# Routing one-hots laid out in token pairs, sums laid out by token, and a second stretch without GpSimd: a hybrid decoder layer on one core

## The chip, the cores and the metric

The kernel runs on one core of one Trainium2 chip. The metric is device time in microseconds (us) of one execution. Before the change the median of 3 runs is 2627.22 us (2626.87 to 2627.82).

## The reference, cut to what matters

One decoder layer for 256 tokens of width 2048, all in float32. A first sub-layer (modulated RMSNorm, a convolution branch and a dilated attention branch, an output projection, a residual) is not touched by the change. The second sub-layer is a retrieval of single-neuron experts: for each token, 8 heads choose 16 experts each out of 128 x 128 by product keys, with softmax weights g, and then

```
u = take(w_up, idx)                      # 128 experts of each token
a = gelu(einsum('td,tkd->tk', x, u))
y = einsum('tk,tkd->td', g * a, take(w_down, idx))
```

where `idx = e1 * 128 + e2` and `w_up`, `w_down` are 16384 x 2048.

## The kernel before, in words

The kernel gathers nothing. It computes the up products of all 16384 experts for all 256 tokens, multiplies them by a dense matrix of routing weights C (expert by token, zero where an expert isn't chosen) and multiplies the result by all of `w_down`. The experts are worked in four quarters q of 32 values of e1 (EQ = 32); within one e1, the 128 values of e2 lie on the partitions.

*Float32 by parts.* A weight half of 128 x 1024 is split into `hi` (a float32r copy, ScalarE, line 84) and `lo` (the rest, raw - hi, line 88, on DVE or GpSimd). A product is then three float32r matmuls: hi x hi, hi x lo, lo x hi. In the up products the weights are the stationary operand (lines 1265 to 1267, tile `aps`, 256 columns each); in the down products C is (parts `cch`, `ccl`; lines 1428 to 1431, tiles `y` and `z`, 512 columns each).

*Order.* Work is a list of units of two halves. A `Stream` emits for each half: `a` (for up units a DVE transpose `wt`, then `hi`) three halves ahead, `b` (`lo`, and for down units `cch` and `ccl`) two ahead, and `mm` (the matmuls). What a half carries as `after` is emitted ahead of the next half's `mm`. `hi` has 4 buffers, `lo` 3, `wt` 2, `cch` and `ccl` 3, the raw weight tile 4; a `lo` therefore waits for the matmuls of three halves before. Each engine runs its own instructions in the order of emission. DMA loads of weights are issued by SyncE, when a raw tile comes free.

*Routing weights.* `gate_c(p)` makes C for two quarters, in two passes p of 32 blocks of 8 tokens (NT = 8). Each step of the generator does three things: `apply` for block b-2 (DVE multiplies the sums into C of one quarter, line 1348; ScalarE copies the other quarter's, line 1353), `build` for block b (DVE: `oh2`, line 1328, a one-hot of e2; `oh1`, line 1330, a one-hot of 64 values of e1; `ohg`, line 1333, `oh1` times three bf16 parts of g), and `product` for block b-1 (line 1342: for each of the 8 tokens three matmuls, stationary `oh2` of 128 columns, moving `ohg` of 64 columns, summed over the parts into the PSUM tile `gps`). In the profile `oh1` and `oh2` are both `oh`. The tiles are laid out [.., key, token], with the 8 tokens innermost, so a matmul, which takes one token, reads every eighth bf16 and writes every eighth float32.

*Where the passes lie.* Pass 0 goes beside the 18 "solo" up units of quarter 1, one step after each half; their `lo` are all on GpSimd. I call this the first stretch. Pass 1 goes beside the down units of quarter 1 for the output columns 1024 to 2047 (d == 1), one step after each half, and two steps more in front; all their `lo` are on GpSimd too (in the quarters 0, 2 and 3, d == 1, those of every unit's first half only). I call it the second stretch. The line that chooses, 1407, is

```
split_b(h, u.raw[...], nc.gpsimd if d == 1 and (q == 1 or n == 0) else nc.vector)
```

Of the kernel before, what the change touches and what calls it, by code (L numbers as in the profile page):

```python
# [14 lines left out]
OP = mybir.AluOpType  # L15
# [3 lines left out]
P = 128  # L19
# [14 lines left out]
EQ = 32  # L34
# [32 lines left out]
def layer_kernel(ctx, tc, x, c, norm1_g, norm2_g, w_ada, b_ada, w_in, conv_dw, conv_db, conv_ln_g,  # L67
# [991 lines left out]
    def open_p2():  # L1059
        pool = p2.enter_context(tc.tile_pool(name="p2", bufs=1))  # L1060
        T2["pool"] = pool
        CB[:] = [pool.tile([P, EQ * T], F32, name=f"C{i}") for i in range(2)]
        T2["keys"], T2["keysT"] = CB[0][:, 0:2048], CB[0][:, 2048:4096]
        nc.gpsimd.dma_start(T2["keys"].rearrange("p (a e) -> p a e", a=16),
                            dap(peer_sub_keys, 0, [[P, P], [P * P, 16], [1, P]]))
        T2["scr"] = CB[1]
        it = pool.tile([P, P, 8], BF, name="iota_rep")
        nc.gpsimd.iota(it, pattern=[[1, P], [0, 8]], base=0, channel_multiplier=0, allow_small_or_imprecise_dtypes=True)
        T2["iota"] = it
        T2["e1T"] = pool.tile([P, T], BF, name="e1T")  # L1070
        T2["e2T"] = pool.tile([P, T], BF, name="e2T")
        T2["gp"] = pool.tile([P, 3, T], BF, name="gp")
# [248 lines left out]
    def gate_c(p):  # L1321
        nb = T // NT
        state = {}

        def build(b):
            ts = slice(b * NT, (b + 1) * NT)
            o2 = T2["pool"].tile([P, P, NT], BF, name="oh2", tag="oh2", bufs=2)
            nc.vector.tensor_tensor(o2, T2["iota"], T2["e2T"][:, None, ts].to_broadcast([P, P, NT]), op=OP.is_equal)
            o1 = T2["pool"].tile([P, 2 * EQ, NT], BF, name="oh1", tag="oh1", bufs=1)
            nc.vector.tensor_tensor(o1, T2["iota"][:, 2 * p * EQ:2 * (p + 1) * EQ, :],  # L1330
                                    T2["e1T"][:, None, ts].to_broadcast([P, 2 * EQ, NT]), op=OP.is_equal)
            og = T2["pool"].tile([P, 3, 2 * EQ, NT], BF, name="ohg", tag="ohg", bufs=2)
            nc.vector.tensor_tensor(og, o1[:, None].to_broadcast([P, 3, 2 * EQ, NT]),  # L1333
                                    T2["gp"][:, :, None, ts].to_broadcast([P, 3, 2 * EQ, NT]), op=OP.mult)
            state["o", b] = o2, og

        def product(b):
            o2, og = state.pop(("o", b))
            ps = T2["ps"].tile([P, 2 * EQ, NT], F32, name="gps", tag="m", bufs=2)
            for t in range(NT):  # L1340
                for i in range(3):
                    nc.tensor.matmul(ps[:, :, t], lhsT=o2[:, :, t], rhs=og[:, i, :, t], start=i == 0, stop=i == 2)  # L1342
            state["p", b] = ps

# [35 lines left out]

    def down_unit(q, d, r):

# [9 lines left out]
        for n in range(2):  # L1392
# [11 lines left out]
            def b(h, rr=rr, n=n):  # L1404
                h.ch = T2["pool"].tile([P, T], F32R, name="cch", tag="cch", bufs=3)
                nc.scalar.copy(*row_views(h.ch, q, rr))  # L1406
                split_b(h, u.raw[:, n * 1024:(n + 1) * 1024], nc.gpsimd if d == 1 and (q == 1 or n == 0) else nc.vector)
                h.cl = T2["pool"].tile([P, T], F32R, name="ccl", tag="ccl", bufs=3)
# [4 lines left out]
            def mm(h, rr=rr):  # L1413
# [28 lines left out]
                for t in range(2):  # L1442
                    for c in range(2):
                        products(h, t, c, (0,), first, False)
                    for c in range(2):
                        products(h, t, c, (1,), False, last)

            h.a, h.b, h.mm = a, b, mm
            h.early_b = d == 1
            if rr == EQ - 1 and not (q == 3 and d == 1):  # L1450
                h.after = [lambda: [y_done(q, d, Y["ps"], t, c) for t in range(2) for c in range(2)]]
# [62 lines left out]
    for q in range(4):  # L1514
# [10 lines left out]
        m1 = len(st.halves)  # L1525
        downs = [down_unit(q, 1, r) for r in range(0, EQ, 2)]
        if q == 1:
# [73 lines left out]
```

## Time and profile before

| | |
|---|---|
| median of 3 runs | 2627.22 us |
| profiled execution | 2627.34 us, its span 2625.6 us |
| TensorE busy (matmul / weight load) | 2549.9 us (97%) / 2195.0 us (84%) |
| DVE, ScalarE, GpSimd busy | 1853.8 (71%), 1134.9 (43%), 603.5 us (23%) |
| `gps` matmuls (line 1342) | 1536, recorded mean 303 ns |
| `lo` on GpSimd from raw down weights | 80, mean 2429 ns |
| `ohg`, `oh` of e2, `oh` of e1 on DVE | 64 each, mean 991, 689, 481 ns |
| DMA | 518.74 MB, 198 GB/s over the span |

Matmuls are pipelined and their recorded ends are modelled: a record of 300 ns can be followed by the next start 100 ns later, so the pace is read from starts. "Busy" is a union of such records. A float32 matmul (not float32r) stands as two records. The profile's times are us from the start of the span; "idle before" names what released an instruction.

### The profile page before, as it was taken

The numbers are of one execution on the slowest core, as the hardware profiler recorded it, in microseconds if no ns is written. First come the engines' busy times: TensorE is split into PE (matmuls) and PEld (weight loads), VectorE is DVE, ScalarE is ACT, GpSimd is POOL, SyncE is SP. The second block draws the span as 40 slices with busy tenths as digits, with TensorE's granted clock in tenths as the row PEclk, the third lists the DMA queues.
The fourth block names the chain that finished last, engine by engine and source line by source line (L and its number), as shares of the span: only waits on it lengthen the run. The fifth ranks groups of instructions, "written<-read, shape, count | busy, mean of one in ns | idle before, by whom it ended". The sixth has DMA issues, their size and how long they took to land.

```text
span 2625.6 us, 39801 instructions
## 1 busy us (share of the span) xinstructions
PE 2549.9 (97%) x15760; PEld 2195.0 (84%) x15760; DVE 1853.8 (71%) x2498; ACT 1134.9 (43%) x1493; POOL 603.5 (23%) x294
## 2 busy tenths in 40 slices
PE   7999899999999999999999999999999999999999
PEld 4677677777766999889999988999888999998877
DVE  2655688785554689875568777777787776667776
ACT  5333354445334444432235555555333344445454
POOL 1000000000000038774423243222144211124023
PEclk9999999999999999999999999999999999999999
DMA  9886346777899787774438856889522577765563
GB/s 317 294 294 240 128 145 217 251 273 272 280 304 257 159 179 165 165 157 94 97 94 243 237 198 204 223 227 244 161 97 90 117 185 185 185 187 194 206 212 124
DMA packets 261179, 518.74 MB, mean 198 GB/s; under 512 B 16400, under 2 KB 57568, under 8 KB 260352
## 3 DMA queue, kind: packets, MB, share of 16 engines
q1 hardware_dynamic: 258912, 507.61, 67.3%
q0 software_dynamic: 2048, 8.58, 0.9%
q8 instruction: 123, 2.02, 0.3%
q14 instruction: 64, 0.52, 0.1%
q10 hardware_dynamic: 32, 0.01, 0.0%
HBM read 511.94 MB, written 4.19 MB: 197 GB/s over the span
## 4 chain that ended last, share of the span: by engine, by line
PE 79%; DVE 4%; POOL 2%; issue 2%; ACT 1%; DMA 1%; SPq 0%; DVEq 0%; POOLq 0%; ACTq 0%
PE aps L1267 7%; PE aps L1265 7%; PE aps L1266 7%; PE gps L1342 7%; PE y L1428 6%; PE y L1429 6%; PE y L1431 6%; PE z L429 5%; PE z L431 5%; PE z L430 5%; PE z L1429 3%; PE z L1431 3%; PE z L1428 3%; POOL lo L88 2%; PE ada L330 2%
## 5 line engine op out<-in xcount | busy, mean ns | idle before, releaser
L88 DVE TENSOR_TENSOR lo<-raw,hi 128x1024 fp32r<-128x1024 f32 x432 | 532.9, 1238 | 369.2 <-issue 104.3
L84 ACT CAST hi<-raw 128x1024 fp32r<-128x1024 f32 x512 | 535.0, 1052 | 519.9 <-PE aps L1266 99.2
L1267 PE MATMUL aps<-h2hi,lo 128*128 128x256 f32 x2048 | 581.2, 284 | 8.7 <-POOL lo L88 8.5
L1265 PE MATMUL aps<-h2hi,hi 128*128 128x256 f32 x2048 | 583.1, 285 | 0.4 <-ACT hi L84 0.4
L1266 PE MATMUL aps<-h2lo,hi 128*128 128x256 f32 x2048 | 579.9, 283 | 0.0
L84 ACT CAST hi<-wt 128x1024 fp32r<-128x1024 f32 x256 | 269.5, 1053 | 515.2 <-DVE wt L1250 339.7
L1267 PEld LDWEIGHTS aps<-h2hi,lo 128*128 128x128 f32 x2048 | 392.9, 192 | 11.3 <-POOL lo L88 11.3
L1265 PEld LDWEIGHTS aps<-h2hi,hi 128*128 128x128 f32 x2048 | 393.7, 192 | 2.4 <-ACT hi L84 0.6
L88 POOL TENSOR_TENSOR lo<-wt,hi 128x1024 fp32r<-128x1024 f32 x116 | 288.1, 2490 | 467.5 <-PE aps L1267 354.2
L1266 PEld LDWEIGHTS aps<-h2lo,hi 128*128 128x128 f32 x2048 | 393.3, 192 | 1.8
L1250 DVE STREAM_TRANSPOSE wt<-raw 128x1024 f32<-128x1024 f32 x256 | 315.9, 1237 | 97.7 <-POOL lo L88 85.5
L1411 DVE TENSOR_TENSOR ccl<-C,cch 128x256 fp32r<-128x256 f32 x256 | 258.7, 1012 | 134.8 <-ACT cch L1406 68.6
L88 POOL TENSOR_TENSOR lo<-raw,hi 128x1024 fp32r<-128x1024 f32 x80 | 194.3, 2429 | 423.4 <-PE y L1429 194.0
L1428 PE MATMUL y<-hi,cch 128*128 128x512 f32 x640 | 254.9, 398 | 0.0
L1429 PE MATMUL y<-lo,cch 128*128 128x512 f32 x640 | 250.2, 391 | 0.0
L1342 PE MATMUL gps<-ohg,oh 128*128 128x64 bf16 x1536 | 199.1, 303 | 8.2 <-DVE ohg L1333 8.1
L1342 PEld LDWEIGHTS <-oh 128*128 128x128 bf16 x1536 | 182.3, 147 | 18.0 <-issue 14.4
L1431 PE MATMUL y<-hi,ccl 128*128 128x512 f32 x640 | 197.4, 390 | 0.0
L88 DVE TENSOR_TENSOR lo<-wt,hi 128x1024 fp32r<-128x1024 f32 x140 | 170.9, 1223 | 29.2 <-PE aps L1267 12.5
L1406 ACT CAST cch<-C 128x256 fp32r<-128x256 f32 x256 | 103.1, 403 | 176.3 <-PE z L1429 102.0
L347 POOL TENSOR_TENSOR acc<-acc,raw 128x512 f32<-128x512 f32 x60 | 101.5, 1691 | 262.6 <-ACT raw L346 225.3
L1429 PE MATMUL z<-lo,cch 128*128 128x512 f32 x384 | 149.5, 389 | 2.2 <-DVE lo L88 2.2
(293 smaller groups left out, 4055.2 us busy)
## 6 DMA issues: line engine op xcount, KB each, us to landing
raw<-in_peer_w_up_dram SPq DMA_DIRECT2D x512, 256.0 KB, 5.8
raw<-in_peer_w_down_dram SPq DMA_DIRECT2D x128, 1024.0 KB, 5.1
raw<-in_w_ada_dram SPq DMA_DIRECT2D x86, 1024.0 KB, 7.0
raw<-in_w_in_dram SPq DMA_DIRECT2D x73, 1024.0 KB, 5.3
raw<-in_w_out_dram SPq DMA_DIRECT2D x64, 256.0 KB, 5.1
raw<-in_peer_w_q_dram SPq DMA_DIRECT2D x64, 256.0 KB, 6.5
raw<-in_w_in_dram SPq DMA_DIRECT2D x22, 512.0 KB, 8.8
raw<-in_w_ada_dram SPq DMA_DIRECT2D x20, 512.0 KB, 5.1
```

What stands on the lines that cost most here:

```text
L84: nc.scalar.copy(h.hi, src)
L88: eng.tensor_tensor(h.lo, src, h.hi.bitcast(F32), op=OP.subtract)
L429: nc.tensor.matmul(z, lhsT=ah, rhs=hi[:, kk], start=first, stop=False)
L1250: nc.vector.transpose(wt.rearrange("p j g a -> p g j a"), u.raw.rearrange("p (g j a) -> p g j a", g=4, a=32)[:, :, n * 8:(n + 1) * 8, :])
L1265: nc.tensor.matmul(z, lhsT=hi[:, jj], rhs=qh["hi"][:, j, :], start=j == 0, stop=False)
L1266: nc.tensor.matmul(z, lhsT=hi[:, jj], rhs=qh["lo"][:, j, :], start=False, stop=False)
L1267: nc.tensor.matmul(z, lhsT=lo[:, jj], rhs=qh["hi"][:, j, :], start=False, stop=j == NK - 1)
L1342: nc.tensor.matmul(ps[:, :, t], lhsT=o2[:, :, t], rhs=og[:, i, :, t], start=i == 0, stop=i == 2)
L1411: nc.vector.tensor_tensor(cl, row, ch, op=OP.subtract)
L1428: nc.tensor.matmul(z, lhsT=ch, rhs=hi, start=first, stop=False)
L1429: nc.tensor.matmul(z, lhsT=ch, rhs=lo, start=False, stop=False)
L1431: nc.tensor.matmul(z, lhsT=cl, rhs=hi, start=False, stop=last)
```

## The change

Three edits.

1. The one-hot tiles are laid out [block of two tokens, key, 2 tokens] instead of [key, 8 tokens]; `iota_rep` shrinks from 8 to 2 copies. A matmul now reads every second bf16. `ohg` is made by three instructions, one for each part of g, instead of one.
2. The PSUM tile `gps` is laid out [token, 64 values of e1] instead of [64 values, token]; a matmul writes 64 neighbouring float32, and `apply` reads through a transposed view.
3. In the second stretch (q == 1, d == 1) all `lo` go to DVE, and every fourth row (r % 4 == 2, n == 1: rows 3, 7, ..., 31) has no `hi`, `lo`, `cch` and `ccl`: its four products are plain float32 matmuls of C and the raw weights, and the raw tile is released by them.

```
-        it = pool.tile([P, P, 8], BF, name="iota_rep")
+        it = pool.tile([P, P, 2], BF, name="iota_rep")
...
+            pairs = lambda v: v.rearrange("p (b t) -> p b t", t=2)
+            nb2, ne = NT // 2, 2 * EQ
+            o2 = T2["pool"].tile([P, nb2, P, 2], BF, name="oh2", tag="oh2", bufs=2)
+            nc.vector.tensor_tensor(o2, T2["iota"][:, None].to_broadcast([P, nb2, P, 2]),
+                                    pairs(T2["e2T"][:, ts])[:, :, None].to_broadcast([P, nb2, P, 2]), op=OP.is_equal)
+            o1 = T2["pool"].tile([P, nb2, ne, 2], BF, name="oh1", tag="oh1", bufs=1)
...
+            og = T2["pool"].tile([P, 3, nb2, ne, 2], BF, name="ohg", tag="ohg", bufs=2)
+            for i in range(3):
+                nc.vector.tensor_tensor(og[:, i], o1, pairs(T2["gp"][:, i, ts])[:, :, None].to_broadcast([P, nb2, ne, 2]),
+                                        op=OP.mult)
...
-            ps = T2["ps"].tile([P, 2 * EQ, NT], F32, name="gps", tag="m", bufs=2)
+            ps = T2["ps"].tile([P, NT, 2 * EQ], F32, name="gps", tag="m", bufs=2)
...
-                    nc.tensor.matmul(ps[:, :, t], lhsT=o2[:, :, t], rhs=og[:, i, :, t], start=i == 0, stop=i == 2)
-            state["p", b] = ps
+                    nc.tensor.matmul(ps[:, t, :], lhsT=o2[:, t // 2, :, t % 2], rhs=og[:, i, t // 2, :, t % 2],
+                                     start=i == 0, stop=i == 2)
+            state["p", b] = ps.rearrange("p t e -> p e t")
...
-    def down_unit(q, d, r):
+    def down_unit(q, d, r, whole=False):
...
-                split_b(h, u.raw[:, n * 1024:(n + 1) * 1024], nc.gpsimd if d == 1 and (q == 1 or n == 0) else nc.vector)
+                split_b(h, u.raw[:, n * 1024:(n + 1) * 1024], nc.gpsimd if d == 1 and q != 1 and n == 0 else nc.vector)
...
+            def mm_whole(h, rr=rr, n=n):
+                for t in range(2):
+                    for c in range(2):
+                        nc.tensor.matmul(Y["ps"][t][c], lhsT=c_row(q, rr)[:, t * P:(t + 1) * P],
+                                         rhs=u.raw[:, n * 1024 + c * 512:n * 1024 + (c + 1) * 512], start=False, stop=rr == EQ - 1)
...
+            if whole and n == 1:
+                h.a, h.b, h.mm, h.rel = None, None, mm_whole, "m"
...
-        downs = [down_unit(q, 1, r) for r in range(0, EQ, 2)]
+        downs = [down_unit(q, 1, r, q == 1 and r % 4 == 2) for r in range(0, EQ, 2)]
```

## Rows read from the trace of the kernel before

**Rows 1.** The page's part 4: chain that ended last, shares of the span.
```profile
PE 79%; DVE 4%; POOL 2%; issue 2%; ACT 1%; DMA 1%; SPq 0%; DVEq 0%; POOLq 0%; ACTq 0%
```

**Rows 2.** Timeline, one period of the first stretch: start us, us, engine, instruction, [idle before].
```profile
1239.64 2.40 POOL L88 TENSOR_TENSOR lo<-wt,hi 128x1024 fp32r<-128x1024 f32 x1 [3.44 <-PE aps L1267]
...
1242.08 1.25 DVE L1250 STREAM_TRANSPOSE wt<-raw 128x1024 f32<-128x1024 f32 x1 [2.37 <-POOL lo L88]
...
1243.25 0.38 DVE L1348 TENSOR_TENSOR C<-gps,C 128x256 f32<-128x256 f32 x1
...
1243.56 0.67 DVE L1328 TENSOR_TENSOR oh<-iota_rep,e2T 128x1024 bf16<-128x1024 bf16 x1
...
1244.15 0.41 DVE L1330 TENSOR_TENSOR oh<-iota_rep,e1T 128x512 bf16<-128x512 bf16 x1
...
1244.60 0.96 DVE L1333 TENSOR_TENSOR ohg<-oh,gp 128x1536 bf16<-128x1536 bf16 x1
...
1245.15 3.08 PE L1342 MATMUL gps<-ohg,oh 128*128 128x64 bf16 x24
...
1245.45 2.41 POOL L88 TENSOR_TENSOR lo<-wt,hi 128x1024 fp32r<-128x1024 f32 x1 [3.41 <-PE aps L1267]
...
1247.98 0.37 PE L1265 MATMUL aps<-h2hi,hi 128*128 128x256 f32 x1
```

**Rows 3.** Windows: stretch and length, busy by engine, PEclk, DMA share, GB/s.
```profile
1168.20:1169.50 1.30, 1.26 (x11) 1.26 (x11) 1.30 (x2) 0.07 (x1) 0.00 (x0) 0.50 0.00 0
...
1171.00:1172.50 1.50, 1.50 (x10) 1.50 (x9) 1.50 (x3) 0.00 (x0) 0.00 (x0) 0.50 0.52 150
```

**Rows 4.** Timeline of TensorE in the second of these windows.
```profile
1171.64 0.41 PE L1267 MATMUL aps<-h2hi,lo 128*128 128x256 f32 x1
...
1171.85 0.41 PE L1265 MATMUL aps<-h2hi,hi 128*128 128x256 f32 x1
```

**Rows 5.** Groups of weight loads by shape: busy, mean ns of one, idle before.
```profile
L1342 PEld LDWEIGHTS <-oh 128*128 128x128 bf16 x1536 | 182.3, 147 | 18.0 <-issue 14.4 <-DVE oh L1328 1.4 <-DVE ohg L1333 0.6
...
L359 PEld LDWEIGHTS gateps<-ones,acc 128*128 128x128 f32 x64 | 8.2, 191 | 0.4
```

**Rows 6.** Timeline of TensorE, a run of one-column float32 products.
```profile
465.98 0.95 PE L359 MATMUL gateps<-ones,acc 128*128 128x1 f32 x8
466.80 0.48 PE L429 MATMUL z<-hi,h1hi 128*128 128x512 f32 x1
```

**Rows 7.** Timeline, one period of the second stretch.
```profile
1999.87 2.41 POOL L88 TENSOR_TENSOR lo<-raw,hi 128x1024 fp32r<-128x1024 f32 x1 [3.33 <-PE y L1429]
...
1999.93 3.12 PE L1342 MATMUL gps<-ohg,oh 128*128 128x64 bf16 x24
...
2000.19 2.36 DVE L1411 TENSOR_TENSOR ccl<-C,cch 128x256 fp32r<-128x256 f32 x1 [1.12 <-ACT cch L1406]
...
2005.64 3.12 PE L1342 MATMUL gps<-ohg,oh 128*128 128x64 bf16 x24
```

**Rows 8.** Line 1411 from 1380 to 1525 us: ns min/median/max, first and last start.
```profile
L1411 DVE TENSOR_TENSOR ccl<-C,cch x29: 418/426/1516, 1381.2 to 1523.7; 128x256 fp32r<-128x256 f32 x29
```

**Rows 9.** Line 1250, up units of quarter 0, 963 to 1160 us.
```profile
L1250 DVE STREAM_TRANSPOSE wt<-raw x63: 1199/1233/1250, 966.0 to 1159.3; 128x1024 f32<-128x1024 f32 x63
```

**Rows 10.** Windows, the same stretch: PE, PEld, DVE, ACT, POOL busy.
```profile
963.00:1160.00 197.00, 187.93 (x1539) 185.09 (x1538) 169.76 (x301) 82.30 (x92) 161.58 (x65) 1.00 0.79 169
```

**Rows 11.** Timeline, a plain float32 product of 512 columns, two records.
```profile
754.80 1.02 PE L929 MATMUL rbp<-rb,ones 128*128 128x512 f32 x2
```

**Rows 12.** Line 929: the length of such a record.
```profile
L929 PE MATMUL rbp<-rb,ones x16: 592/592/592, 729.6 to 2463.6; 128*128 128x512 f32 x16
```

**Rows 13.** Groups of DVE instructions by shape, float32 with two operands.
```profile
L88 DVE TENSOR_TENSOR lo<-raw,hi 128x1024 fp32r<-128x1024 f32 x432 | 532.9, 1238 | 369.2 <-issue 104.3 <-ACT hi L84 103.4 <-PE zv L558 43.8
...
L1304 DVE TENSOR_TENSOR C<-C,hrow 128x512 f32<-128x512 f32 x16 | 10.9, 680 | 0.0
```

**Rows 14.** Timeline of DVE, the start of the second stretch.
```profile
1890.76 2.62 DVE L1330 TENSOR_TENSOR oh<-iota_rep,e1T 128x512 bf16<-128x512 bf16 x1
```

More of the change, by code (lines that the diff above doesn't have):

```diff
@@ L1066, in open_p2 @@
         T2["scr"] = CB[1]
-        it = pool.tile([P, P, 8], BF, name="iota_rep")
-        nc.gpsimd.iota(it, pattern=[[1, P], [0, 8]], base=0, channel_multiplier=0, allow_small_or_imprecise_dtypes=True)
+        it = pool.tile([P, P, 2], BF, name="iota_rep")
+        nc.gpsimd.iota(it, pattern=[[1, P], [0, 2]], base=0, channel_multiplier=0, allow_small_or_imprecise_dtypes=True)
         T2["iota"] = it
@@ L1325, in build @@
         def build(b):
+            pairs = lambda v: v.rearrange("p (b t) -> p b t", t=2)
             ts = slice(b * NT, (b + 1) * NT)
[L1327 to L1334, printed above, removed]
+            nb2, ne = NT // 2, 2 * EQ
[3 more added lines that the diff above has]
+            o1 = T2["pool"].tile([P, nb2, ne, 2], BF, name="oh1", tag="oh1", bufs=1)
+            nc.vector.tensor_tensor(o1, T2["iota"][:, None, p * ne:(p + 1) * ne].to_broadcast([P, nb2, ne, 2]),
+                                    pairs(T2["e1T"][:, ts])[:, :, None].to_broadcast([P, nb2, ne, 2]), op=OP.is_equal)
+            og = T2["pool"].tile([P, 3, nb2, ne, 2], BF, name="ohg", tag="ohg", bufs=2)
+            for i in range(3):
+                nc.vector.tensor_tensor(og[:, i], o1, pairs(T2["gp"][:, i, ts])[:, :, None].to_broadcast([P, nb2, ne, 2]),
+                                        op=OP.mult)
             state["o", b] = o2, og
```

## The prediction

> **What bounds the kernel now.** I read the chain of waits first: TensorE holds 79% of it, DVE 4%, GpSimd 2% [rows 1]. So a change pays where it shortens TensorE's own work, or costs where it makes TensorE wait. Next the timeline of one period in each of the two places that the change touches.
>
> *First stretch* (the routing sums of pass 0 beside the solo up units, 32 bursts). One period runs from one GpSimd `lo` to the next, 1239.64 to 1245.45: 5.81 us [rows 2]. In it TensorE does a burst of 24 `gps` products, 1245.15 to 1247.98 = 2.83 us or 118 ns a product, and 24 up products in the other 2.98 us; it has no gap. But it isn't alone. GpSimd's `lo` takes 2.40 us; when it ends, DVE starts its transpose `wt` (1.25), then the apply step (0.38), `oh` (0.67), `oh` (0.41), `ohg` (0.96), and ends at 1245.56, just as the next `lo` starts. DVE and GpSimd follow each other and together fill the period that TensorE sets.
>
> *Second stretch* (pass 1 beside the down products of columns 1024 to 2047 of quarter 1, again 32 bursts). The period is 1999.93 to 2005.64 = 5.71 us [rows 7]: the same burst of 2.83, then 12 down products of 512 columns in 2.88. Here too GpSimd makes every `lo` (2.41), and DVE's `ccl`, which starts 0.32 us after it, lasts 2.36 us and ends with it; without GpSimd beside it `ccl` takes 0.43 [rows 7, 8].
>
> **What paces a `gps` product.** 64 columns against 128 weights should be quick. Twelve products of 512 columns in 2.88 us (240 ns) and 24 of 256 in 2.98 (124 ns) give 0.45 ns a column, so 64 columns would come to 124 - 192 x 0.45, some 40 ns [rows 2, 7]. They take 118. It isn't the array's clock: from 1168.20 to 1169.50, after TensorE had stood idle for the first build, the granted clock was 0.50 (1.2 GHz of 2.4) and 11 products ran in 1.30 us, 118 ns each, just as at full clock; straight after, still at 0.50, the products of 256 columns were 0.21 us apart instead of 0.12, as an array at half clock should have them [rows 3, 4]. So the pace is set by what feeds the array or takes from it, and there this product is unlike all others: both operands are read with a step of 16 bytes and the sums are written with a step of 32. The change makes the steps 4 bytes and the sums dense.
>
> What is left then? The weights. Eight pairs with 128 float32 weights and one column take 465.98 to 466.80, 103 ns each [rows 6]. The load of `oh` is recorded at 147 ns against 191 for theirs [rows 5], 44 less, so 59 ns by the weights; with a few ns for the handover I take 65. The ends are 40 (columns alone) and 118 (no change); 65 is nearest to the weights' row.
>
> The Trainium skill has a rule against this: "TensorE: Matmul & The Clock Gate", section on LDWEIGHTS, puts a load at the number of weight columns over 1.2, 107 ns for 128 columns whatever their layout. The 103 ns of the float32 pair agree with it, the shorter record of the bf16 load speaks against it; by it the burst would shrink to 2.57 us only, and the time would be about 2616.
>
> **Part by part.**
>
> *Burst.* 24 x 0.065 = 1.56 us for 2.83: 1.27 us less on TensorE, 64 times. All of it would be 81 us.
>
> *Builds on DVE.* The two `oh` keep element counts and instruction counts; `ohg` is now three instructions of 512 elements instead of one of 1536. The second `oh` is an instruction of that size (0.41), so 3 x 0.41 = 1.23 for 0.96, +0.27 a step. That inner runs of 2 go as fast as runs of 8 no row shows: between 0 and double (the rival below). I take 0, as the type and the element step are the same.
>
> *First stretch after.* TensorE alone: 5.81 - 1.27 = 4.54. Now the cover matters. An instruction of DVE that reads two SBUF operands stands while GpSimd's `lo` runs [rows 7, 8]; the transpose does not: 63 of them took 1.20 to 1.25 while GpSimd was busy 161.58 of 197 us [rows 9, 10]. So the build, from start to start 0.59 + 0.45 + 3 x 0.45 = 2.39 [rows 2], must lie outside the `lo`, while `wt` and the apply step can lie beside it: 1.25 + 0.38 = 1.63 fits into 2.40. Of a blocked instruction 0.15 us run under the cover (`ccl` ends 0.28 after `lo`, alone it takes 0.43). The bound is 2.40 + 2.39 - 0.15 = 4.64 to 4.79 without that: I take 4.72, above TensorE's 4.54. Gain 32 x (5.81 - 4.72) = 34.9 us.
>
> *Second stretch after.* No GpSimd work, so `ccl` is 0.43 again. DVE per ordinary half: `lo` 1.24 [rows 13], `ccl` 0.43, apply 0.38 [rows 2], build 0.67 + 0.41 + 1.23: 4.36. TensorE: 5.71 - 1.27 = 4.44. They all but meet, and DVE must wait for its `lo` buffer first; I take 4.47. In every fourth half (8 of 32) the products are float32: 4 products that are recorded as two instructions each; such a record of 512 columns follows the one before it by 1.02 - 0.59 = 0.43 us [rows 11, 12] (8 matmuls stand as 16 records). 8 x 0.43 = 3.44 and an allowance of 0.1 for the handover stand for the 2.88 of before: the half takes 1.56 + 3.54 = 5.10. DVE has 2.69 and ScalarE one cast and one copy less there, a reserve for the next halves. Gain 24 x (5.71 - 4.47) + 8 x (5.71 - 5.10) = 29.8 + 4.9 = 34.7 us.
>
> *At nothing:* the apply and the copy read PSUM with a step now: they already step through `C`, and at double they would add 0.3 us beside `lo` in the first stretch (hidden) and on DVE in the second (24 x 0.3 = 7 us at worst). The raw tile of a float32 half is released by its products, two to three halves later than by `lo`; four tiles of two halves each cover some 37 us of work, far more than the halves that the release is late. The shorter iota is off the path. At the start of the second stretch an `oh` was held to 2.62 us by `lo` [rows 14]; that may give back 2 us, uncounted.
>
> *Sum.* 34.9 + 34.7 = 69.6 us. The profiled execution took 2627.34 (span 2625.6), 0.1 above the median, so: 2627.3 - 69.6 = **2558 us**. With 40 ns the first stretch stays at 4.65 by the port and the second at 4.42 by DVE (4.50 in the float32 halves): 37 + 41 = 78, 2549. With 80 ns TensorE sets 4.90 in the first, 4.80 and 5.46 in the second: 29 + 24 = 53, 2574.
>
> **Rivals.**
>
> *The port takes the first stretch's gain.* When TensorE is quicker, `lo` is released earlier, at the end of each half's products, and can slip in between the five instructions of a build. A caught piece waits 2.40 us, TensorE's next burst with it, and that period is 7.2 us. If it hits every second period the mean is (4.7 + 7.2)/2 = 5.95, so no gain: 2627 - 34 = 2593. For it: the `oh` of 2.62 us [rows 14], and that `ohg` is now three pieces. Against: by the order above the last piece starts some 0.3 us before `lo` is due. The skill's "SBUF — State Buffer", section "SBUF: two separate sides", calls it an exclusive lock that goes to whoever starts first and is kept for the whole instruction; the blocked `ccl` agrees.
>
> *The weights set the pace whatever the steps.* The float32 pair's 103 ns for 128 weights [rows 6] hold for bf16 too: burst 2.47, first stretch 5.45, second 5.35 and 6.01: 11.5 + 6.2 = 18, so 2609. At 118 nothing is gained and the float32 halves cost 8 x 0.66 = 5.3: 2633.
>
> *Slower: runs of two lose DVE's double pace.* bf16 goes at 0.96/1536 = 0.62 ns an element [rows 2], float32 at (1.238 - 0.680)/512 = 1.09 [rows 13]. At float32 pace a build is 1.24 + 0.68 + 3 x 0.68 = 3.96. First stretch: 2.40 + 3.96 - 0.15 = 6.21, 32 x 0.40 = +12.8. Second: DVE 6.01 in ordinary halves, 24 x 0.30 = +7.2, less 4.9. Sum +15: 2642. It decides from a build of 3.56 us (5.81 - 2.40 + 0.15). For it: no instruction of before has runs of two. Against: the element step is 1 as before.
>
> **Chances.** Forecast's mechanism (2549 to 2574) 0.62; port 0.14; weights 0.13 (about a third of it ends within 0.2%, a third slower); double pace lost 0.07; the rest 0.04. Range for 8 in 10: 2545 to 2606. Within 0.2% (5 us), about what a measurement of this kernel can tell from no change: 0.05. Slower 0.12, faster 0.83.
>
> **What would show it.** Right: `gps` bursts of some 1.6 us; three `ohg` of 0.41 and `oh` of 0.67 and 0.41; `ccl` at 0.43 and no GpSimd in the second stretch; periods near 4.7 in both, 5.1 for a float32 half, whose products are 0.43 us apart. Wrong: bursts above 2 us; builds above 3 us; in the first stretch periods that alternate between short and long with `oh` or `ohg` of 2.5 us or more.

## The result, and the profile after

The changed kernel takes **2518.31 us** (median of 4 runs, 2516.41 to 2522.80) against 2627.05 (2625.95 to 2627.82) for the kernel before: ratio 0.9587, 95% interval 0.9576 to 0.9599. It is 109 us faster; the forecast was 70 us, 2558, and the range began at 2545. So the sign was right and the size was not. The span of the profiled execution is 2516.4 us, 109.2 less than before.

**Where the 109 us come from.** The apply step (DVE, `C<-gps,C`) runs once for each burst, so its first and last record in a stretch measure the stretch. First the kernel before, then the one after; the columns are start us, us, engine, instruction, [idle before].

```profile
1172.32 0.38 DVE L1348 TENSOR_TENSOR C<-gps,C 128x256 f32<-128x256 f32 x1
...
1352.91 0.42 DVE L1348 TENSOR_TENSOR C<-gps,C 128x256 f32<-128x256 f32 x1 [5.36 <-PE gps L1342]
...
1905.47 0.41 DVE L1348 TENSOR_TENSOR C<-gps,C 128x256 f32<-128x256 f32 x1
...
2083.46 0.41 DVE L1348 TENSOR_TENSOR C<-gps,C 128x256 f32<-128x256 f32 x1
```

```profile
1172.44 0.39 DVE L1354 TENSOR_TENSOR C<-gps,C 128x256 f32<-128x256 f32 x1
...
1309.97 0.42 DVE L1354 TENSOR_TENSOR C<-gps,C 128x256 f32<-128x256 f32 x1 [0.58 <-PE gps L1347]
...
1854.63 0.42 DVE L1354 TENSOR_TENSOR C<-gps,C 128x256 f32<-128x256 f32 x1
...
1971.65 0.41 DVE L1354 TENSOR_TENSOR C<-gps,C 128x256 f32<-128x256 f32 x1
```

| stretch (31 intervals each) | before | after | gain | forecast |
|---|---|---|---|---|
| first | 180.59 | 137.53 | 43.1 | 34.9 |
| between the two | 552.56 | 544.66 | 7.9 | 0 (2 named, uncounted) |
| second | 177.99 | 117.02 | 61.0 | 34.7 |

What lies ahead of the first and behind the second gives 2.7 us back. (The forecast counted 32 periods. The boundaries are steps of DVE; from burst to burst the time between the two falls by 4.6 us, 546.72 to 542.12.)

**The burst.** TensorE in the second stretch, the rows that answer to [rows 7]: an ordinary half runs from one `gps` to the next, 1888.22 to 1891.80; the `x8` row is a float32 half.

```profile
1888.22 0.90 PE L1347 MATMUL gps<-ohg,oh 128*128 128x64 bf16 x24
1888.96 0.48 PE L1435 MATMUL y<-hi,cch 128*128 128x512 f32 x1
...
1891.80 0.90 PE L1347 MATMUL gps<-ohg,oh 128*128 128x64 bf16 x24
1892.53 3.68 PE L1458 MATMUL y<-raw,C 128*128 128x512 f32 x8
1896.05 0.89 PE L1347 MATMUL gps<-ohg,oh 128*128 128x64 bf16 x24
```

24 products start 1888.22 and the next work starts 1888.96: 0.74 us, 30 ns a product, where it was 118. I had forecast 65, with 40 as the lower end. The load of the weights shrank too; the group by shape (busy, mean ns of one, idle before) answers to [rows 5], 147 there:

```profile
L1347 PEld LDWEIGHTS <-oh 128*128 128x128 bf16 x1536 | 54.8, 98 | 36.7 <-issue 25.6 <-DVE ohg L1338 6.0 <-DVE oh L1331 1.9
```

The float32 half is 1892.53 to 1896.05 = 3.52 beside its burst, 0.44 a record, as forecast. `ccl` takes 0.42 and comes again 3.88 us later, which is DVE's pace in ordinary halves, and `ohg` is three pieces of 0.42 that start 0.34 apart (DVE, the same stretch; a record `x3` is the three together):

```profile
1890.06 0.42 DVE L1418 TENSOR_TENSOR ccl<-C,cch 128x256 fp32r<-128x256 f32 x1
...
1893.94 0.42 DVE L1418 TENSOR_TENSOR ccl<-C,cch 128x256 fp32r<-128x256 f32 x1
...
1895.66 1.10 DVE L1338 TENSOR_TENSOR ohg<-oh,gp 128x512 bf16<-128x512 bf16 x3
```

TensorE is what bounds this stretch: its bursts start 3.57, 3.57, 3.57 and 4.25 us apart all through it, 3.74 on average, and the window (PE, PEld, DVE, ACT, POOL busy, then PEclk) has no idle time, no GpSimd and full clock.

```profile
1855.00:1970.00 115.00, 115.00 (x1080) 83.83 (x1077) 111.29 (x232) 43.43 (x76) 0.00 (x0) 1.00 0.46 138
```

**The first stretch** is two stretches. From the ninth on, 21 intervals are 4.28 us long, and the last two, which have no build left, 3.12 and 1.00. One settled period (answering to [rows 2]; DVE, GpSimd and the burst):

```profile
1231.35 1.49 PE L1347 MATMUL gps<-ohg,oh 128*128 128x64 bf16 x24
1231.65 2.58 POOL L88 TENSOR_TENSOR lo<-wt,hi 128x1024 fp32r<-128x1024 f32 x1 [1.70 <-PE aps L1267]
1231.88 1.24 DVE L1250 STREAM_TRANSPOSE wt<-raw 128x1024 f32<-128x1024 f32 x1
1233.04 0.38 DVE L1354 TENSOR_TENSOR C<-gps,C 128x256 f32<-128x256 f32 x1
1233.35 1.43 DVE L1331 TENSOR_TENSOR oh<-iota_rep,e2T 128x1024 bf16<-128x1024 bf16 x1
1234.70 0.41 DVE L1334 TENSOR_TENSOR oh<-iota_rep,e1T 128x512 bf16<-128x512 bf16 x1
1235.15 1.09 DVE L1338 TENSOR_TENSOR ohg<-oh,gp 128x512 bf16<-128x512 bf16 x3
...
1235.93 2.59 POOL L88 TENSOR_TENSOR lo<-wt,hi 128x1024 fp32r<-128x1024 f32 x1 [1.70 <-PE aps L1267]
```

`lo` runs 1231.65 to 1234.23; `wt` and the apply step lie beside it, `oh` stands until it ends (1.43 for 0.67), and then the build follows. That is the picture of the forecast. But the first eight intervals are 5.74, 7.35, 3.52, 7.03, 3.52, 7.02, 3.52 and 5.76, mean 5.43: here GpSimd's `lo` catches the `ohg` pieces, and TensorE stands for 2.29 us within its burst.

```profile
1181.21 3.24 DVE L1338 TENSOR_TENSOR ohg<-oh,gp 128x512 bf16<-128x512 bf16 x3
1181.58 2.59 POOL L88 TENSOR_TENSOR lo<-wt,hi 128x1024 fp32r<-128x1024 f32 x1 [1.29 <-PE aps L1267]
...
1184.50 0.83 PE L1347 MATMUL gps<-ohg,oh 128*128 128x64 bf16 x22 [2.29 <-DVE ohg L1338]
```

### The profile page after: what moved, and what is told of

It is laid out like the page before. It is cut to its first block, busy times and chain, and to the rows that moved or that the text cites. A ratio compares the mean times of both kernels' runs of the same rounds, so it can differ in the third digit from the quotient of the medians.

```text
span 2516.4 us, 39750 instructions
## 1 busy us (share of the span) xinstructions
PE 2426.6 (96%) x15728; PEld 2056.6 (82%) x15728; DVE 1854.2 (74%) x2642; ACT 1120.8 (45%) x1477; POOL 530.3 (21%) x262
## 4 chain that ended last, share of the span: by engine, by line
PE 71%; DVE 10%; POOL 3%; issue 2%; DMA 1%; ACT 1%; SPq 0%; DVEq 0%; POOLq 0%; ACTq 0%
PE aps L1267 6%; PE aps L1265 6%; PE aps L1266 6%; PE y L1435 6%; PE y L1436 6%; PE y L1438 5%; PE z L429 5%; PE z L431 4%; PE z L430 4%; PE z L1436 3%; PE z L1438 3%; PE z L1435 3%; POOL lo L88 3%; DVE wt L1250 2%; PE ada L330 2%
## 5 line engine op out<-in xcount | busy, mean ns | idle before, releaser
L88 DVE TENSOR_TENSOR lo<-raw,hi 128x1024 fp32r<-128x1024 f32 x456 | 561.8, 1237 | 376.3 <-issue 112.6
L84 ACT CAST hi<-raw 128x1024 fp32r<-128x1024 f32 x504 | 526.6, 1051 | 520.6 <-PE zv L559 103.1
L1418 DVE TENSOR_TENSOR ccl<-C,cch 128x256 fp32r<-128x256 f32 x248 | 198.9, 803 | 96.7 <-PE z L1438 57.6
L1435 PE MATMUL y<-hi,cch 128*128 128x512 f32 x608 | 241.1, 397 | 0.0
L1436 PE MATMUL y<-lo,cch 128*128 128x512 f32 x608 | 237.3, 390 | 0.0
L1438 PE MATMUL y<-hi,ccl 128*128 128x512 f32 x608 | 187.6, 390 | 0.0
L88 POOL TENSOR_TENSOR lo<-raw,hi 128x1024 fp32r<-128x1024 f32 x48 | 117.0, 2436 | 245.9 <-PE z L1436 123.6
L1435 PE MATMUL z<-hi,cch 128*128 128x512 f32 x384 | 149.5, 389 | 1.0 <-ACT cch L1413 1.0
L1438 PEld LDWEIGHTS y<-hi,ccl 128*128 128x128 f32 x608 | 114.2, 188 | 24.4
```

The costliest lines, as they stand in the source:

```text
L84: nc.scalar.copy(h.hi, src)
L88: eng.tensor_tensor(h.lo, src, h.hi.bitcast(F32), op=OP.subtract)
L1418: nc.vector.tensor_tensor(cl, row, ch, op=OP.subtract)
L1435: nc.tensor.matmul(z, lhsT=ch, rhs=hi, start=first, stop=False)
L1436: nc.tensor.matmul(z, lhsT=ch, rhs=lo, start=False, stop=False)
L1438: nc.tensor.matmul(z, lhsT=cl, rhs=hi, start=False, stop=last)
```

## The experiments

All times below are medians; the kernel before took 2626 to 2627 beside each. Lengths of stretches, pitches and windows are those of the one execution that was profiled. The pitch of a `gps` product is the time from the first product of a burst to the next work, over 24.

### One part at a time

**e1_sums**: only the sums made dense, the one-hots as before.

```diff
-            ps = ...tile([P, 2 * EQ, NT], F32, name="gps", ...)
+            ps = ...tile([P, NT, 2 * EQ], F32, name="gps", ...)
...
-                    nc.tensor.matmul(ps[:, :, t], lhsT=o2[:, :, t], rhs=og[:, i, :, t], ...)
+                    nc.tensor.matmul(ps[:, t, :], lhsT=o2[:, :, t], rhs=og[:, i, :, t], ...)
```

> The kernel before with the sums alone laid out by token (gps writes 64 neighbouring float32); one-hots stay eight tokens deep, GpSimd keeps its lo. Theory S (the 32-byte step of the sums paced the product at 118 ns): bursts of 0.73 us as in the changed kernel, time near that of both layouts together, 2545 to 2560 us. Theory W (the 16-byte step of the stationary one-hots paced it) and theory M (that of the moving ones): bursts stay 2.83 us, time 2627 us. If sums and operands share it: a burst in between.

Measured 2691.80, ratio 1.0248 (1.0231 to 1.0266): slower, which no theory had. Bursts of TensorE, then windows of both stretches and of the 3.3 us behind the first of these bursts:

```profile
1241.67 3.13 PE L1342 MATMUL gps<-ohg,oh 128*128 128x64 bf16 x24
1244.56 0.56 PE L1265 MATMUL aps<-h2hi,hi 128*128 128x256 f32 x1
...
1249.00 3.13 PE L1342 MATMUL gps<-ohg,oh 128*128 128x64 bf16 x24
```

```profile
1180.00:1380.00 200.00, 200.00 (x1417) 198.66 (x1416) 97.51 (x142) 42.69 (x67) 71.70 (x30) 0.84 0.35 79
1940.00:2130.00 190.00, 189.84 (x1025) 162.57 (x1024) 129.25 (x143) 51.66 (x85) 67.41 (x28) 0.85 0.26 78
1244.60:1247.90 3.30, 3.30 (x17) 3.30 (x16) 3.25 (x5) 0.00 (x0) 0.00 (x0) 0.50 0.28 56
```

The first stretch of the kernel before:

```profile
1180.00:1340.00 160.00, 160.00 (x1323) 158.73 (x1322) 94.45 (x138) 40.52 (x63) 66.55 (x28) 1.00 0.40 93
```

The burst stays at 2.89 us: the operands alone hold the pace. But the granted clock is 0.84 and 0.85 where before it was 1.00. These are means of the two levels: behind the burst at 1241.67 it was 0.50 (1.2 GHz), and the 24 up products take 1244.56 to 1249.00 = 4.44 us in place of 2.98 [rows 2]. The other products get slower with the clock; a burst at 0.50 does not [rows 3].

**e2_pairs**: only the one-hots in token pairs; the sums keep their step of 32 bytes.

```diff
+                    nc.tensor.matmul(ps[:, :, t], lhsT=o2[:, t // 2, :, t % 2], rhs=og[:, i, t // 2, :, t % 2], ...)
```

> The kernel before with the one-hots alone in token pairs (4-byte step); the sums keep their 32-byte step. Theory S: bursts stay 2.83 us and the time 2627 us, or a few us more for the three ohg. Theories W and M: bursts of 0.73 us, time 2545 to 2560 us.

2589.75, ratio 0.9858 (0.9841 to 0.9874). The pitch is 1.33/24 = 55 ns:

```profile
1241.88 1.52 PE L1346 MATMUL gps<-ohg,oh 128*128 128x64 bf16 x24
1243.21 0.36 PE L1265 MATMUL aps<-h2hi,hi 128*128 128x256 f32 x1
```

So the sums' step alone costs 25 ns a product, once the operands are quick. The first stretch is 136.52 us, as short as after's: the dense sums gain nothing there. The second stretch is 183.4, longer than before, as in the next experiment, which shows why.

**e3_layouts**: one-hots and sums as in the change; the second stretch keeps GpSimd's low parts and has no float32 rows.

```diff
-                split_b(h, ..., nc.gpsimd if d == 1 and q != 1 and n == 0 else nc.vector)
+                split_b(h, ..., nc.gpsimd if d == 1 and (q == 1 or n == 0) else nc.vector)
```

> Both layouts, and the second stretch as before: GpSimd makes all its lo, no float32 rows. All theories: bursts 0.73 us and a first stretch of 4.28 us a period, gain 32 x 1.53 = 49 us. Second stretch: if GpSimd's lo (2.40) and DVE's two-operand instructions (ccl 0.42, build 2.05) exclude each other, a period of 4.7 to 4.9, gain 26 to 32 us: 2546 to 2552 us. If they do not, TensorE sets 3.57, gain 68 us: 2510 us, and the third edit was worth nothing.

2587.21, ratio 0.9848 (0.9831 to 0.9864), only 39 us of the 109, and 35 above the 2546 to 2552 that were expected if `lo` and DVE's instructions exclude each other. The first stretch is 139.57 us, near after's. The second is 181.7 for 177.99 before, though a burst with its operands ready is 2.1 us shorter: GpSimd's `lo` now catches the build, and TensorE waits for the build. One such case, and the window of the stretch:

```profile
1983.40 2.54 POOL L88 TENSOR_TENSOR lo<-raw,hi 128x1024 fp32r<-128x1024 f32 x1 [1.22 <-ACT C L1357]
1983.77 3.12 DVE L1337 TENSOR_TENSOR ohg<-oh,gp 128x512 bf16<-128x512 bf16 x3
...
1986.28 2.00 PE L1346 MATMUL gps<-ohg,oh 128*128 128x64 bf16 x24 [2.65 <-DVE ohg L1337]
```

```profile
1865.00:2020.00 155.00, 116.67 (x938) 90.24 (x936) 123.12 (x185) 48.42 (x80) 64.73 (x27) 0.87 0.30 90
```

TensorE is busy for 116.67 of 155 us; the intervals alternate near 4.76 and 7.0 to 7.4. The forecast had this rival, but for the first stretch, with 5.95 on average; here it is 5.86. Not all of that is waiting: the granted clock is 0.87. Of 5.86 us TensorE is idle for 1.45 and busy for 4.41, with work that takes 3.57 in after at full clock, so some 0.8 us an interval come with the slower clock, which falls behind such waits (0.50 from 1904.40 to 1907.70, after TensorE had waited for the `ohg` before).

**e4_second**: only the second stretch's part of the change: its low parts on DVE, each fourth row's half as float32 products; the one-hots and sums of before.

```diff
-                split_b(h, ..., nc.gpsimd if d == 1 and (q == 1 or n == 0) else nc.vector)
+                split_b(h, ..., nc.gpsimd if d == 1 and q != 1 and n == 0 else nc.vector)
...
-        downs = [down_unit(q, 1, r) for r in range(0, EQ, 2)]
+        downs = [down_unit(q, 1, r, q == 1 and r % 4 == 2) for r in range(0, EQ, 2)]
```

> The third edit alone: no GpSimd in the second stretch, every fourth row float32, both layouts as before. Theory of the prediction (TensorE's 118 ns products set the period, not the port): 8 float32 halves cost 0.66 us each and nothing is gained: 2630 to 2633 us. Rival (GpSimd's hold on DVE cost time in the second stretch already before): below 2622 us.

2629.47, ratio 1.0011 (1.0001 to 1.0020), just under the 2630 to 2633 expected. With slow bursts TensorE is the bound, and the eight float32 halves cost 0.67 us each (6.37 from burst to burst for 5.70), 5.4 together; the rival holds at the start of the stretch alone, where TensorE waits 0.76 us for `ohg` and in the kernel before waited 3.35. So the layouts alone bring 39 us, this edit alone loses 3, and both together win 109: with quick bursts GpSimd's low parts would be the bound of the second stretch, and this edit takes them away.

### What a gps product waits for

The kernel after, with the step of one operand (or of both) changed. The diffs are of the operand views; the tiles and the iota change with them (tokens innermost in eights: a step of 16 bytes; in fours: 8 bytes).

**e5_stat** and **e6_mov**: one operand in pairs, the other in eights.

```diff
 e5_stat:
-  rhs=og[:, i, t // 2, :, t % 2]
+  rhs=og[:, i, :, t]
 e6_mov:
-  lhsT=o2[:, t // 2, :, t % 2]
+  lhsT=o2[:, :, t]
```

> The kernel after, with only its stationary one-hots (oh2) in token pairs; the moving ones (oh1, ohg) step by 16 bytes again, the sums stay dense. Theory M (the moving operand's 16-byte step is what holds 118 ns a gps product): burst of 24 stays near 2.8 us, and the clock falls as it did with dense sums alone, time 2640 to 2700. Theory W (the stationary operand's step, read by the weight load): burst near 0.73 us and the time that of after, 2515 to 2525. If each operand holds about half, 55 to 75 ns a product, burst 1.3 to 1.8, time 2530 to 2570.

> The reverse: only the moving one-hots (oh1, ohg) in token pairs, the stationary ones (oh2) step by 16 bytes, sums dense. Theory M: burst near 0.73 us, time 2515 to 2525. Theory W: burst near 2.8 us, time 2640 to 2700 with the fallen clock. Each about half: 1.3 to 1.8 us, 2530 to 2570. The weight load's own record (97 ns in after, 146 before) should be 146 here and 97 in the run above, whichever theory holds.

e5_stat: 2655.56, ratio 1.0125 (1.0108 to 1.0142), pitch 2.71/24 = 113 ns, and the granted clock falls here too, to a mean of 0.94 in the first stretch (0.92 in the second). e6_mov: 2547.88, 0.9703 (0.9687 to 0.9720), pitch 1.47/24 = 61 ns at full clock. The weight load's record is 116 ns in e5_stat and 167 in e6_mov, not the 97 and 146 expected: it is longer with the stationary operand's step, but not set by it alone. Burst and window of e5_stat, then the burst of e6_mov:

```profile
1201.26 2.96 PE L1347 MATMUL gps<-ohg,oh 128*128 128x64 bf16 x24
1203.97 0.37 PE L1266 MATMUL aps<-h2hi,hi 128*128 128x256 f32 x1
```

```profile
1180.00:1350.00 170.00, 170.00 (x1368) 168.75 (x1368) 148.88 (x141) 40.76 (x64) 71.74 (x29) 0.94 0.39 87
```

```profile
1882.25 1.64 PE L1347 MATMUL gps<-ohg,oh 128*128 128x64 bf16 x24
1883.72 0.47 PE L1434 MATMUL y<-hi,cch 128*128 128x512 f32 x1
```

**e9_quads**, **g1_mov4**, **g2_stat4**: groups of four tokens for both operands, for the moving one, for the stationary one.

```diff
 e9_quads:
-  lhsT=o2[:, t // 2, :, t % 2], rhs=og[:, i, t // 2, :, t % 2]
+  lhsT=o2[:, t // 4, :, t % 4], rhs=og[:, i, t // 4, :, t % 4]
 g1_mov4: the rhs alone
 g2_stat4: the lhsT alone
```

> The kernel after with the one-hots in groups of four tokens: both operands step by 8 bytes in place of 4. If the price of a product grows with the step's bytes (30 ns at 4, 118 at 16): 55 to 65 ns, burst 1.3 to 1.6 us, the second stretch about 0.7 us longer in each half with a gate step, 32 of these, time 2535 to 2545. If there is a step (free up to 8 bytes): burst 0.73, time 2515 to 2522 or a little less, since VectorE's inner runs are longer.

> The kernel after, with only its moving one-hots (oh1, ohg) in groups of four tokens, so an 8-byte step; the stationary ones stay in pairs (4 bytes), sums dense. With both at 8 bytes a gps product took 61 ns, with only the stationary ones at 16 bytes 61 too, with only the moving ones at 16 bytes 113. Theory M (a product takes 64 columns times a price that grows with the moving operand's step): 61 ns here, burst 1.46 us, 2540 to 2546. Theory W (at 8 bytes the stationary operand alone holds 61): 30 ns here, burst 0.73, 2515 to 2522.

> The reverse: only the stationary one-hots (oh2) at an 8-byte step, the moving ones in pairs. Theory M: 30 ns or a little more, burst 0.73 to 0.9 us, 2515 to 2525. Theory W: 61 ns, burst 1.46, 2540 to 2546.

e9_quads: 2544.52, 0.9691 (0.9675 to 0.9708), pitch 61. g1_mov4: 2540.97, 0.9675 (0.9634 to 0.9717), pitch 60. g2_stat4: 2528.81, 0.9629 (0.9550 to 0.9707), pitch 0.80/24 = 33. (g1 and g2: two runs each, so g2's interval takes in that of after.) g2's median stands 10 us above after, and its profiled run 15, although its bursts are nearly as short: in that run the first stretch alternates for longer and is 149.3 us. So the moving operand holds the 61 ns. Bursts of g1_mov4 and g2_stat4:

```profile
1894.36 1.63 PE L1350 MATMUL gps<-ohg,oh 128*128 128x64 bf16 x24
1895.80 0.47 PE L1438 MATMUL y<-hi,cch 128*128 128x512 f32 x1
```

```profile
1892.62 0.96 PE L1349 MATMUL gps<-ohg,oh 128*128 128x64 bf16 x24
1893.42 0.48 PE L1437 MATMUL y<-hi,cch 128*128 128x512 f32 x1
```

**e10_cols**: each product takes the 128 columns of a pair.

```diff
-  nc.tensor.matmul(ps[:, t, :], lhsT=..., rhs=og[:, i, t // 2, :, t % 2], ...)
+  nc.tensor.matmul(ps[:, t // 2 * 2:t // 2 * 2 + 2, :]..., lhsT=..., rhs=og[:, i, t // 2]..., ...)
```

> The kernel after, but each gps product takes 128 columns (both tokens of a pair) in place of 64; the routing sums are then not the reference's. Theory C (30 ns is the time of the 64 columns): 56 ns a product, burst 1.3 us, 0.6 us more in each half of the second stretch that has a gate step, 32 of these, and little in the first stretch where VectorE sets the pace (PE 2.96 + 1.34 = 4.30 against 4.28): 2535 to 2545. Theory L (30 ns is a handover or the weight load): burst stays 0.73 to 0.85 us, time 2516 to 2522.

2538.36, 0.9668 (0.9651 to 0.9684), pitch 1.32/24 = 55 ns:

```profile
1884.46 1.50 PE L1347 MATMUL gps<-ohg,oh 128*128 128x128 bf16 x24
1885.78 0.48 PE L1435 MATMUL y<-hi,cch 128*128 128x512 f32 x1
```

64 columns more cost 25 ns, but the edit changes the moving operand's step too: the two columns of a pair lie side by side, 2 bytes apart in place of 4. Were the step alone the price, 128 columns at 2 bytes would take what 64 take at 4, 30 ns; they take 55, 0.43 a column. At that price 64 columns are 27 or 28 of after's 30 ns, so the columns make nearly all of it (an estimate: 64 columns at 2 bytes were not run). Together:

| what is slow | pitch, ns |
|---|---|
| nothing (after) | 30 |
| stationary operand, 8 bytes / 16 bytes | 33 / 61 |
| moving operand, 8 bytes / 16 bytes | 60 / 113 |
| sums, 32 bytes | 55 |
| both operands 16 bytes, sums dense / 32 bytes | 120 / 118 |

Within some 7 ns the slowest of them sets the pitch; they do not add up.

### What bounds the stretches now

**e7_nowhole**: no float32 rows, all low parts of the second stretch on DVE.

```diff
-        downs = [down_unit(q, 1, r, q == 1 and r % 4 == 2) for r in range(0, EQ, 2)]
+        downs = [down_unit(q, 1, r) for r in range(0, EQ, 2)]
```

> The kernel after without its float32 rows: all low parts of the second stretch on VectorE, no row as float32 products. From after's trace PE needs 0.73 + 2.84 = 3.57 us for an ordinary half and 4.25 for a float32 one (mean over four 3.74), VectorE 3.88 and 2.7. Theory V (the float32 rows pay because they take VectorE's work away, and the gain of the layouts comes from the absence of GpSimd's low parts): all halves at VectorE's 3.88, 32 x 0.14 = 4.5 us over after, 2521 to 2525, VectorE busy all through the stretch. Theory R (the float32 rows themselves carry a good part of the gain that the layouts alone didn't show): 2540 or more. A cheaper stretch, 2513 (TensorE at 3.57), if VectorE's pieces overlap better than their sum.

2528.06, 0.9621 (0.9608 to 0.9634), 10 us more than after. The intervals of the second stretch are 3.86 or 3.87 up to the last four, DVE's pace as expected, and the stretch is 123.72 us, 6.7 more (not 4.5: in after the first twelve run at 3.5 on average, ahead of TensorE's 3.74). Another 2.1 us are the first stretch's, which this edit doesn't touch and which alternated for two steps longer.

**e8_solo_dve**: no low part on GpSimd in the first stretch either (`busy` puts it there, `none` on DVE).

```diff
-    solo = [up_unit(1, r, busy) for r in range(nsolo)]
+    solo = [up_unit(1, r, none) for r in range(nsolo)]
```

> The kernel after, but in the first stretch (the units with a gate step) the low parts are VectorE's too, GpSimd has none there. Theory X (the period of 4.28 us is GpSimd's low part, 2.35 after VectorE's last one-hot piece, and then VectorE's build of 1.93, one after the other): without the lock VectorE's own work is 1.16 + 0.31 + 0.62 + 0.45 + 1.01 = 3.55 us from start to start, and with the low part of 1.16 it is 4.71: 34 x 0.43 = 15 us slower than after, 2531 to 2535. Theory Y (GpSimd's use of the port costs VectorE more than its low part is worth): the period falls under 4.28, 2505 to 2515.

2519.37, 0.9590 (0.9577 to 0.9603), the same as after. The period is 4.66, as the first theory had it, and even, up to the last two intervals:

```profile
1230.78 1.24 DVE L1250 STREAM_TRANSPOSE wt<-raw 128x1024 f32<-128x1024 f32 x1
...
1235.44 1.23 DVE L1250 STREAM_TRANSPOSE wt<-raw 128x1024 f32<-128x1024 f32 x1
```

What both theories missed is that after has its 4.28 only in 21 of 31 intervals. With eight at 5.43 its stretch is 137.5 us, e8's 138.5.

**f1_split** and **f2_split6**: each low part of the first stretch but the first three split, 640 columns on GpSimd and 384 on DVE behind the build; f2 also has float32 rows in 5 halves for 8.

```diff
+    GCOLS = 640
...
+                g = GCOLS if pool_lo == "parts" and 2 * r + n > LB else 1024
...
+                sub_(nc.gpsimd, slice(0, g))
+                rest_lo.append(lambda: sub_(nc.vector, slice(g, 1024)))
...
-    solo = [up_unit(1, r, busy) for r in range(nsolo)]
+    solo = [up_unit(1, r, "parts") for r in range(nsolo)]
...
-            h.after.append(lambda: gate_step(0))
+            h.after.append(lambda: (gate_step(0), [rest_lo.pop(0)() for _ in rest_lo[:]]))
...
-        downs = [down_unit(q, 1, r, q == 1 and r % 4 == 2) for r in range(0, EQ, 2)]
+        downs = [down_unit(q, 1, r, q == 1 and r % 6 == 2) for r in range(0, EQ, 2)]     (f2 only)
```

> The kernel after, with each low part of the first stretch split: 640 of its 1024 columns on GpSimd, 384 on VectorE, and these behind the gate step's build. Theory X: GpSimd's part takes 2.35 x 0.625 = 1.47 us, just what VectorE's transpose and apply take beside it (1.47), then build 1.93 and its own part 0.43: period 3.84 in place of 4.28, TensorE needing 3.70; 34 x 0.44 = 15 us less, 2502 to 2506. If GpSimd's shorter part starts later (its buffer comes free with the product of an earlier low part) nothing is won: 2516 to 2520.

> The split low parts of the run before, and in the second stretch a float32 row in each sixth unit's half, 5 of 32 in place of 8: TensorE 3.57 + 0.68 x 5/32 = 3.68 us a half, VectorE 3.88 - 1.18 x 5/32 = 3.70, against 3.74 with 8 of 32: 32 x 0.04 = 1.3 us less than the split alone, 2500 to 2505. Where the two engines stand equal each waits for the other at times: up to 3 us more than the split alone.

2535.07 (0.9644; 0.9631 to 0.9657) and 2535.81 (0.9653; 0.9640 to 0.9666): 17 us slower than after, a miss. GpSimd's part is released by a product of TensorE as before, and now falls on DVE's own part or on the build:

```profile
1232.88 1.64 POOL L1264 TENSOR_TENSOR lo<-wt,hi 128x640 fp32r<-128x640 f32 x1 [2.07 <-PE aps L1277]
1233.02 1.92 DVE L1264 TENSOR_TENSOR lo<-wt,hi 128x384 fp32r<-128x384 f32 x1
```

1.92 for 0.55: one catch in most periods, many of which are 5.5 us; the stretch is 156.0 in f1 (152.4 in f2). In f2 the second stretch is 122.1 us for 117.0 as well: fewer float32 halves leave DVE behind.

**g3_late**, timed again as **h0_late4**: the low parts of the first 4 solo units on DVE; **h1_late2**: of the first 2.

```diff
-    solo = [up_unit(1, r, busy) for r in range(nsolo)]
+    solo = [up_unit(1, r, busy if r >= 4 else none) for r in range(nsolo)]
```

> The kernel after, but the low parts of the first 4 of its 18 solo units are VectorE's, those of the others GpSimd's as in after. In after the first eight steps of the first stretch take 5.43 us on average (3.52 and 7.03 in turn, the long one with a piece of ohg caught by GpSimd's low part), the steps behind them 4.28. Theory T (the alternation belongs to the start of the stretch): eight steps at 4.66 and 23 at 4.28 or less at the end, the first stretch about 4 us shorter, 2513 to 2517. Theory D (it begins wherever GpSimd's low parts begin, and lasts eight steps): 2519 to 2524.

> The version with the first 4 solo units' low parts on VectorE, timed: the first stretch 131 us from its first to its last apply step, as in its first look, against 137.5 in after, so 2511 to 2514, ratio to before 0.956 to 0.957. If the look was a lucky case: the alternation of 3.52 and 7.03 comes back and the time is 2518.

> The same with the first 2 solo units only. Theory T (the alternation belongs to the start of the stretch and one or two steps at VectorE's even pace are enough to pass it): steps of 4.66 become 4.28, some 1.5 us less than with four, 2509 to 2513. Theory S (the lead that TensorE has at the start must be used up first): the alternation comes back for some steps, 2514 to 2520.

h0_late4: 2512.26 (2509.88 to 2513.11), ratio to before 0.9561 (0.9547 to 0.9574), against 0.9587 (0.9576 to 0.9599) for after: **6 us faster than after**, in intervals that just don't overlap, and the quickest version here. (g3_late, two runs: 2511.52, 0.9563, 0.9516 to 0.9610.) Its first and last apply step:

```profile
1172.19 0.42 DVE L1354 TENSOR_TENSOR C<-gps,C 128x256 f32<-128x256 f32 x1
...
1303.45 0.42 DVE L1354 TENSOR_TENSOR C<-gps,C 128x256 f32<-128x256 f32 x1 [0.58 <-PE gps L1347]
```

131.3 us for 137.5. The intervals begin 4.66, 4.66, 5.70, 3.52, 5.78 and are 4.28 from then on, but for the last two. h1_late2 gives 2518.80, 0.9592 (0.9579 to 0.9605), and after's intervals from the first to the last: units are split two halves ahead and the first apply comes two steps late, so its four low parts are made before the first interval that counts. It can't tell its two theories apart. A later start of GpSimd's low parts leaves three uneven intervals for eight: shown is that the alternation mostly belongs to the start. Why it dies out is not shown, nor what sets its length, which is ten intervals in e3_layouts and e7_nowhole and 17 in g2_stat4.

## Why the prediction was wrong in size, point by point

**The failed steps: the price of a product after the change, and DVE's work in a half.** The first: "with a few ns for the handover I take 65", from the 103 ns of a float32 one-column pair less 44 for the shorter load. It measured 30, and e10_cols shows that the 64 columns make nearly all of it. The weights' row was the wrong neighbour: a load is recorded at 98 ns while products follow each other at 30, so the length of its record is no pace, and in the loads that were compared, dtype and step differed at once. The lower end of 40, from columns, was itself 10 too high: it took 0.45 ns a column from products of 256 and 512 float32-type columns and put the rest down as a constant.

Put right alone, this price does not make up the miss. With 0.73 us for a burst the forecast's first stretch stays at 4.65 by the port, its ordinary half at 4.42 by DVE, and its float32 half falls to 0.73 + 3.54 = 4.27. That gains 37.1 and 24 x 1.29 + 8 x 1.44 = 42.5, so 2548: still within the range, and 29 us above the 2518 measured, of which 18.5 lie in the second stretch, 6 in the first and the rest outside both. The second step that failed is DVE's 4.36 in an ordinary half. It adds the lengths of records, but they start sooner after each other: 3.87 in all, 1.02 for 1.23 in the `ohg` pieces and 2.85 for 3.13 in the rest. And each half was bounded by itself, with the reserve of the float32 halves named and not counted. DVE runs ahead, so its mean over four halves counts, (3 x 3.87 + 2.40)/4 = 3.50, and that lies under TensorE's 3.74. From 5.71 to 3.74 in 31 intervals is 61.1 us; the stretch gained 61.0. The two errors hid each other: with DVE's 3.87 and a product of 65 ns TensorE's 4.44 and 5.10 would have been the bound, and the gain 35, as forecast.

**What the pace of before was made of.** The forecast named the three steps together and could not weigh them. Right: it was no matter of the clock, nor of columns. The runs say that the moving operand's 16 bytes alone made 113 of the 118; the stationary operand's (61) and the sums' (55) lay below it, and each would have become the bound had it been left. So all three had to change.

The Trainium skill bears on this table: "Advanced Engine Details and Errata", Memory Cachelines, gives SBUF lines of 16 bytes, full performance from two hits in a line, and PSUM lines of 8 bytes with a loss for sums that are not contiguous. The sums' row agrees, and so do the stationary operand's (33 ns at 8 bytes, 61 at 16). The moving operand's does not: at a step of 8 bytes a line of 16 is hit twice, and it still took 60 ns for 30. The rival taken from the Trainium skill's "TensorE: Matmul & The Clock Gate", LDWEIGHTS (128 columns over 1.2, 107 ns), is refuted by a pair of 30 ns with 128 weights.

**First stretch.** Right in kind: in the settled part DVE's build and GpSimd's `lo` exclude each other and TensorE waits, at 4.28 for 4.72. Of the 0.44, 0.34 are the three `ohg` pieces: they start 0.34 apart, not 0.45 as two instructions of different lines had shown. These 21 intervals gain 32.1 us. Another 6.8 of the 43.1 come from the last two, in which no build is left (4.12 us for 10.88), and which the forecast counted like the others. At the start the forecast's port rival took part of it back: 8 of 31 intervals alternate as it said (3.52 and 7.03, mean 5.27, where it had 4.7 and 7.2). The eight take 43.46 us (47.64 before) for 8 x 4.28 = 34.2, so it cost 9 us; it had been given 0.14 as an all-or-nothing case.

**Second stretch.** `ccl` at 0.42, no GpSimd, a float32 half at 0.44 a record: as forecast. TensorE takes 3.57 in an ordinary half and 4.25 in a float32 one. The forecast saw the two engines meet at 4.4; without the float32 rows DVE is the bound at 3.87 (e7_nowhole), with them TensorE is at 3.74. That the edit is worth so much (e3 to after: 69 us) was not seen: its gain was put to the quick burst, and the runs show that with GpSimd's low parts in place the quick burst gains nothing there.

**Refuted rivals.** Inner runs of two keep DVE's double pace (`oh` 0.67 and 0.41). The weights did not set the pace.

**Uncounted.** 7.9 us between the stretches, of which the forecast had named 2. They come with the third edit: in e4_second, which has it alone, these stretches lie 544.29 us apart, in e3_layouts, which lacks it, 551.29. In the kernel before GpSimd's `lo` held the first build, `oh` [rows 14] and the `ohg` behind it, and TensorE stood idle; the window shows it (columns as above):

```profile
1893.00:1896.50 3.50, 0.16 (x2) 0.14 (x1) 3.47 (x3) 1.83 (x3) 2.44 (x2) 1.00 0.64 192
```

That wait was 3.35 us and is 0.23 in after. With it go 3.1 of the 4.6 us from burst to burst; the other 3.3 of the 7.9 lie in where the apply steps stand behind their bursts, and so between this row of the table and its neighbours.

## What to carry to other kernels

In this kernel the price of a small matmul was about the largest of three: its columns, and what the steps of the operands and of the sums cost. Before a bound is taken from a neighbouring row, look whether dtype, step and column count differ at once, and take the lower end from columns alone. When one term is set to its lower end, look which other term then holds the sum, and size an engine's work from start to start, not by adding lengths of records. Edits that are worth little one by one can be worth most together, when each takes away the wait that the other would leave: ask of each edit what is the next bound without it. Where two engines share a port, the mean of the pattern counts, not its settled period: list all intervals of the stretch.

## What the runs showed of the hardware that was not expected

- A faster write of the sums made the kernel 2.5% slower: with slow moving reads and dense sums (e1_sums, and e5_stat) the granted clock fell to means of 0.84 to 0.94 in stretches where TensorE had next to no idle time, with 0.50 straight behind a burst, while with the sums' step of 32 bytes bursts of the same length, 2.83 us, were followed by 1.00. What makes the difference was not found.
- The price of a moving operand grows nearly with its step: 30, 60 and 113 ns at 4, 8 and 16 bytes for 64 bf16 columns (at 4 bytes the columns' own time, by the estimate above, is as long). The stationary operand is cheaper at the same step: 33 at 8 bytes, 61 at 16.
- Under GpSimd's `lo` DVE's low part of float32 is held like the one-hots (1.92 for 0.55 in f1_split); the transpose and the apply step, which reads PSUM, are not.
